# Differential attention: the weighted difference of the two softmaxes on GpSimd in two operations

## The chip, the cores and the metric

The kernel runs on one core of a Trainium2 chip. The metric is the time of one execution in microseconds (us) on the device. Three runs of the kernel before gave 3536.76, 3540.02 and 3542.56 us, the median is 3540.02.

The engines have short names in the rows: PE is TensorE (matmuls; PEld is its weight load), DVE is VectorE, ACT is ScalarE, POOL is GpSimd, SP starts most transfers.

## The reference

Two layers of a hybrid backbone run on 128 prompt tokens and 1024 latent tokens, all in float32. The second layer mixes a gated linear recurrence with differential attention: 4 heads, each with two sets of queries and keys of 64 columns, and values of 128 columns. Latent tokens see 128 context keys and their own 1024. What matters here:

```python
def diff_attention(q, keys, vals, lam):
    ...
    def block(qi):
        s = jnp.einsum('bhqpd,bhkpd->bhpqk', qi, keys).astype(F32) * scale
        p = jax.nn.softmax(s, axis=-1)
        w = p[:, :, 0] - lam * p[:, :, 1]
        return jnp.einsum('bhqk,bhkv->bhqv', w.astype(vals.dtype), vals)
...
    out_c = head_rms(o_c, p['diff_norm']) * (1.0 - lam_init)
```

lam is one number, worked out from the weights. Its value does not depend on the tokens.

## The kernel before

The layers run as stages, each on all 1152 tokens in nine tiles of 128. A scheduler writes the order of every engine's instructions from the program text, in which some parts are marked urgent. Each engine then works through its own order and waits for what the next instruction needs. An order is fixed: what stands behind a waiting instruction on its engine waits too.

The stage of the change is the attention of the latent tokens (`attention`, line 1303). It lasts from about 2310 to 2633 us and works on 32 blocks, numbered 1 to 32 here: eight blocks of 128 queries for each of four heads. One block goes like this.

- `scores` (L1328): for each of the two sets p, four matmuls into a PSUM tile s of 128x1024. There are two such tiles, so a set's scores can start when the exponential of the same set, one block earlier, has read its tile. The last 128 keys come from `tails` (L1313), for two blocks at once.
- `softmax` (L1199): VectorE takes the maximum of s (L1205) and joins that of the tail (L1207). ScalarE writes the exponentials into p, a tile of 128x1152, in two pieces, and adds each up on the way (L1214). The sums are joined and inverted (L1216, L1217). Neither set is divided by its sum yet. The tiles of the first set exist three times, those of the second twice.
- `weigh` (L1220): r2 becomes the factor for the second set, relative to the first (L1227). Then the combination: p1 = p2 * r2 + p1, on VectorE (L1228). The two softmaxes are urgent, these two lines are not.
- `values` (L1334), written in the program one block later: nine transposes of p1 (L1340) in three groups of three, each copied out of PSUM (ScalarE, VectorE, ScalarE), and nine matmuls with the values, each in two passes (L1344). `attn_tokens` scales the output by r1 (L1234).

After eight blocks (four at the end) the head's rows are normed and transposed back (`attn_out`, L1251), and written to DRAM or, for the last head, to x3.

Matmuls of the output projection are put between the blocks (`mix_group`, L205 to L207: three matmuls and one accumulation on VectorE, L1002, or a first copy on ScalarE). Their weights dl and half of their inputs mxl are made on GpSimd by a subtraction (L218). The weights of an adaLN projection are streamed meanwhile (`ada`, L384). When attention is done, the projection of the last head's rows runs (tile d), then the norm of nine token tiles and the last FFN.

The same `weigh` serves the prompt's 128 tokens (tag "p", tiles of 128x128).

Of the kernel before, what the change touches and what calls it, by code (L numbers as in the profile page):

```python
# [14 lines left out]
ALU = mybir.AluOpType  # L15
# [179 lines left out]
class Kern:  # L195
# [1024 lines left out]
    def weigh(self, pool, scores, r1, tag, bufs=2):  # L1220

        nc = self.nc
        r2 = pool.tile([P, 1], F32, tag="r2" + tag, name="r2")
        with self.urgent():
            p1, s1 = self.softmax(pool, scores(0), "p0", r1, bufs)
            p2, _ = self.softmax(pool, scores(1), "p1", r2)
        nc.vector.tensor_scalar(r2, r2, self.nlam, s1, ALU.mult, ALU.mult)  # L1227
        nc.vector.scalar_tensor_tensor(p1, p2, r2, p1, ALU.mult, ALU.add)  # L1228
        return p1

    def attn_tokens(self, ps, r1, ob, ss, junk):
# [394 lines left out]
```

## Time and profile before

| | |
|---|---|
| median of three runs | 3540.02 us |
| profiled execution | 3542.27 us |
| its span, first to last instruction | 3540.3 us |
| TensorE busy | 3333.9 us, 94% |
| VectorE busy | 1889.5 us, 53% |
| ScalarE busy | 1355.0 us, 38% |
| GpSimd busy | 880.6 us, 25% |
| mean granted clock of TensorE | 0.971 |

The shares are means over stages with different limits. A table of busy time by stretches tells what limits one of them; a list of waits tells which instruction ended an engine's idle time; the timeline gives the start and duration of single instructions. Durations of TensorE's matmuls overlap, so the distance from one start to the next is what they cost.

### The profile page before, as it was taken

To read this page: it belongs to the slowest core of one execution; us is meant where nothing else is said; L and a number is where in the kernel's file an instruction comes from. 1 tells how busy PE (TensorE), PEld (TensorE's weight loads), DVE (VectorE), ACT (ScalarE), POOL (GpSimd) and SP (SyncE) were. 2 spreads that over 40 slices of the span, in tenths; PEclk is the share of its full clock that TensorE was granted. 3 is DMA by queue.
4 is the path that set the end of the run, shared out by engine and by line. 5 is a ranking of instruction groups with operands and counts; after the bars stand their busy time and mean duration, and the time that the engine had idled before them with its cause. 6 is when DMAs were issued, how large, how long until landed. Compare 5 with 4: busy or idle time off the path is not lost.

```text
span 3540.3 us, 55870 instructions
## 1 busy us (share of the span) xinstructions
PE 3333.9 (94%) x23022; PEld 3022.1 (85%) x23022; DVE 1889.5 (53%) x3342; ACT 1355.0 (38%) x2414; POOL 880.6 (25%) x596
## 2 busy tenths in 40 slices
PE   5999999888699999999999999989988999999998
PEld 2999899756589999999988998957777999999997
DVE  5658997487662333433372246547777233343334
ACT  5334333453453222322254434446565322232223
POOL 2422320012242221322240003311125221232214
PEclk7999999999799999999999999989998999999999
DMA  6445334484231110111143324384123110111113
GB/s 216 140 138 153 115 108 142 174 295 157 71 96 39 46 37 30 54 42 42 31 148 115 122 82 133 104 285 114 51 83 108 48 36 25 54 48 47 37 30 137
DMA packets 272700, 348.08 MB, mean 98 GB/s; under 512 B 14354, under 2 KB 231597, under 8 KB 266302
## 3 DMA queue, kind: packets, MB, share of 16 engines
q1 hardware_dynamic: 269294, 334.82, 29.8%
q0 software_dynamic: 3152, 9.70, 0.9%
q8 instruction: 181, 2.97, 0.4%
q14 instruction: 73, 0.60, 0.1%
HBM read 266.58 MB, written 77.89 MB: 97 GB/s over the span
## 4 chain that ended last, share of the span: by engine, by line
PE 79%; DVE 8%; DMA 6%; ACT 3%; POOL 2%; issue 2%; SPq 0%; POOLq 0%; DVEq 0%; ACTq 0%
PE g L206 8%; PE g L207 8%; PE g L205 8%; PE a L205 7%; PE a L206 7%; PE a L207 7%; PE d L205 5%; PE d L206 5%; PE d L207 5%; DMA adaw<-in_ada_w 2%; PE b L1344 1%; DVE f L442 1%; PE s L1328 1%; PE w L205 1%; PE ad L384 1%
## 5 line engine op out<-in xcount | busy, mean ns | idle before, releaser
L206 PE MATMUL g<-hTl,whi 128*128 128x388 f32 (+2 forms) x1728 | 590.3, 342 | 2.3 <-POOL hTl L218 2.3
L205 PE MATMUL g<-hTh,whi 128*128 128x388 f32 (+2 forms) x1728 | 589.0, 341 | 2.3 <-ACT hTh L445 2.3
L207 PE MATMUL g<-hTh,wlo 128*128 128x388 f32 (+2 forms) x1728 | 588.1, 341 | 0.0
L206 PE MATMUL a<-hTl,whi 128*128 128x388 f32 (+2 forms) x1248 | 426.3, 342 | 3.4 <-POOL hTl L218 2.8
L205 PE MATMUL a<-hTh,whi 128*128 128x388 f32 (+2 forms) x1248 | 426.8, 342 | 0.9 <-ACT po L1430 0.5
L207 PE MATMUL a<-hTh,wlo 128*128 128x388 f32 (+2 forms) x1248 | 422.7, 341 | 0.0
L1002 DVE TENSOR_TENSOR acc<-d,acc 128x512 f32<-128x512 f32 x288 | 197.7, 688 | 330.7 <-PE d L207 329.2
L1104 POOL TENSOR_TENSOR ta<-ta,tg 128x386 f32<-128x386 f32 x132 | 135.6, 1027 | 922.4 <-ACT tg L1103 886.4
L205 PEld LDWEIGHTS g<-hTh,whi 128*128 128x128 f32 x1728 | 327.4, 189 | 6.7 <-ACT hTh L445 2.9
L206 PEld LDWEIGHTS g<-hTl,whi 128*128 128x128 f32 x1728 | 327.0, 189 | 6.7 <-POOL hTl L218 3.0
L207 PEld LDWEIGHTS g<-hTh,wlo 128*128 128x128 f32 x1728 | 326.9, 189 | 2.0
L205 PE MATMUL d<-dh,ah 128*128 128x512 f32 x792 | 312.6, 395 | 1.1 <-DVE acc L1002 1.1
L206 PE MATMUL d<-dl,ah 128*128 128x512 f32 x792 | 312.0, 394 | 0.0
L207 PE MATMUL d<-dh,al 128*128 128x512 f32 x792 | 311.9, 394 | 0.0
L476 ACT ACTIVATE tg<-g,cols,cols 128x386 f32<-128x386 f32 x132 | 88.8, 672 | 503.5 <-PE g L207 503.4
L218 POOL TENSOR_TENSOR wlo<-wraw,whi 128x1024 fp32r<-128x1024 f32 x90 | 218.3, 2426 | 160.6 <-ACT whi L211 159.7
L218 POOL TENSOR_TENSOR dl<-draw,dh 128x1024 fp32r<-128x1024 f32 x60 | 149.1, 2486 | 403.1 <-ACT dh L211 402.9
L206 PEld LDWEIGHTS a<-hTl,whi 128*128 128x128 f32 x1248 | 235.9, 189 | 11.3 <-POOL hTl L218 4.6
L205 PEld LDWEIGHTS a<-hTh,whi 128*128 128x128 f32 x1248 | 236.2, 189 | 9.7 <-issue 2.9
L477 DVE SCALAR_TENSOR_TENSOR tg<-g,cols,tg 128x386 f32<-128x386 f32 x132 | 81.8, 620 | 300.8 <-ACT tg L476 300.8
L207 PEld LDWEIGHTS a<-hTh,wlo 128*128 128x128 f32 x1248 | 235.8, 189 | 4.1 <-issue 1.6
L211 ACT ACTIVATE whi<-wraw 128x1024 fp32r<-128x1024 f32 x145 | 152.8, 1053 | 180.2 <-DMA wraw<-in_ffn_up 62.2
(429 smaller groups left out, 7050.3 us busy)
## 6 DMA issues: line engine op xcount, KB each, us to landing
adaw<-in_ada_w SPq DMA_DIRECT2D x48, 1024.0 KB
wraw<-in_ffn_up SPq DMA_DIRECT2D x88, 512.0 KB
draw<-in_ffn_down SPq DMA_DIRECT2D x44, 512.0 KB
wraw<-in_w_in_even SPq DMA_DIRECT2D x32, 512.0 KB
wraw<-in_w_in_odd SPq DMA_DIRECT2D x24, 512.0 KB
hgT<-po SPq DMA_DIRECT2D x16, 576.0 KB
ymid<-acc SPq DMA_DIRECT2D x18, 512.0 KB
y<-ymid SPq DMA_DIRECT2D x18, 512.0 KB
```

What stands on the lines that cost most here:

```text
L205: mm(out, lh, rh, start=start, stop=False)
L206: mm(out, lh, rl, start=False, stop=False)
L207: mm(out, ll, rh, start=False, stop=stop)
L211: eng.activation(out, in_, AF.Copy)
L218: eng.tensor_tensor(out, a, b, ALU.subtract)
L384: nc.tensor.matmul(ps[32 * n:32 * n + 32], self.csx[:, k, :], w[:, n, :], start=(k == 0), stop=(k == KD - 1))
L442: nc.vector.tensor_scalar(f[:, j], pt[:, 128 * j:128 * j + 128], mod[:, 1, g, k:k + 1], mod[:, 0, g, k:k + 1], ALU.mult, ALU.add)
L476: nc.scalar.activation(out, ps[:, 1:1 + n], AF.Identity, scale=w[1], bias=b)
L477: nc.vector.scalar_tensor_tensor(out, ps[:, 0:n], w[0], out, ALU.mult, ALU.add)
L1002: nc.vector.tensor_tensor(acc[:, i, s], ps, acc[:, i, s], ALU.add)
L1104: nc.gpsimd.tensor_tensor(ta, ta, tg, ALU.mult)
L1328: nc.tensor.matmul(s[:, k0:k0 + 512], q[:, p, 128 * t:128 * t + 128], kx[:, p, k0:k0 + 512], start=(x == 0), stop=(x == 1))
```

## The change

For the latent tokens (tag "s") the combination leaves VectorE. GpSimd multiplies the second set's exponentials by r2 in place, and then adds them to the first set's. The prompt's four combinations stay on VectorE.

```diff
         nc.vector.tensor_scalar(r2, r2, self.nlam, s1, ALU.mult, ALU.mult)
-        nc.vector.scalar_tensor_tensor(p1, p2, r2, p1, ALU.mult, ALU.add)
+        if tag == "s":
+            nc.gpsimd.tensor_scalar(p2, p2, r2, None, ALU.mult)
+            nc.gpsimd.tensor_tensor(p1, p1, p2, ALU.add)
+        else:
+            nc.vector.scalar_tensor_tensor(p1, p2, r2, p1, ALU.mult, ALU.add)
         return p1
```

Lines behind it move down by four: the transposes are L1344 in the kernel after, the value matmuls L1348, the scores L1332. The product is L1229, the sum L1230. The scheduler also writes a new order of the whole stage.

GpSimd before, from the end of the first adaLN piece to the end of attention; this is all that stands there. Numbers in names tell buffers apart.

```order
L218 TENSOR_TENSOR dl<-draw,dh 128x1024
L218 TENSOR_TENSOR mxl<-mxl,mxh 128x1152 x2
L218 TENSOR_TENSOR dl<-draw,dh 128x1024 x2
L218 TENSOR_TENSOR mxl<-mxl,mxh 128x1152
L218 TENSOR_TENSOR dl<-draw,dh 128x1024
L218 TENSOR_TENSOR mxl<-mxl,mxh 128x1152
L218 TENSOR_TENSOR dl<-draw,dh 128x1024
L218 TENSOR_TENSOR mxl<-mxl,mxh 128x1152
L218 TENSOR_TENSOR dl<-draw,dh 128x1024
```

GpSimd now, around blocks 16 and 17 (p_23452 is block 16's first set, p_23529 and p_23543 are block 17's two, p_23596 and p_23610 block 18's):

```order
L218 TENSOR_TENSOR dl<-draw,dh 128x1024
L1230 TENSOR_TENSOR p_23452<-p_23452,p_23466 128x1152
L218 TENSOR_TENSOR mxl<-mxl,mxh 128x1152
L218 TENSOR_TENSOR dl<-draw,dh 128x1024
L1229 TENSOR_SCALAR p_23543<-p_23543,r_23523 128x1152
L1229 TENSOR_SCALAR p_23610<-p_23610,r_23590 128x1152
L1230 TENSOR_TENSOR p_23529<-p_23529,p_23543 128x1152
L1230 TENSOR_TENSOR p_23596<-p_23596,p_23610 128x1152
```

Two products now stand ahead of block 17's sum, and three subtractions of the projection stand between block 16's product and block 17's. Further on, around block 28 (p_24325 and p_24339; block 29 is p_24400 and p_24414):

```order
L1229 TENSOR_SCALAR p_24264<-p_24264,r_24244 128x1152
L1230 TENSOR_TENSOR p_24250<-p_24250,p_24264 128x1152
L1229 TENSOR_SCALAR p_24339<-p_24339,r_24319 128x1152
L1229 TENSOR_SCALAR p_24414<-p_24414,r_24394 128x1152
L218 TENSOR_TENSOR mxl<-mxl,mxh 128x1152
L1230 TENSOR_TENSOR p_24325<-p_24325,p_24339 128x1152
L1230 TENSOR_TENSOR p_24400<-p_24400,p_24414 128x1152
L1229 TENSOR_SCALAR p_24481<-p_24481,r_24461 128x1152
```

Two products and a subtraction stand between block 27's sum and block 28's.

TensorE now, ahead of block 17's transposes (p_23529); the scores are the first set's of block 20:

```order
L1317 MATMUL b<-kh,q 128x128
L1317 MATMUL b<-kl,q 128x128
L1332 MATMUL s<-kh,q 128x512
L1332 MATMUL s<-kl,q 128x512
L1332 MATMUL s<-kh,q 128x512
L1332 MATMUL s<-kl,q 128x512
L1344 MATMUL b<-ident,p_23529 128x128 x6
L1332 MATMUL s<-kh,q 128x512
L1332 MATMUL s<-kl,q 128x512
```

The transposes stand right behind that set of scores. Block 28's follow the first set of block 31 with three more matmuls between:

```order
L1332 MATMUL s<-kh,q 128x512
L1332 MATMUL s<-kl,q 128x512
L1332 MATMUL s<-kh,q 128x512
L1332 MATMUL s<-kl,q 128x512
L207 MATMUL w<-dh,mxl 128x512
L205 MATMUL w<-dh,mxh 128x512
L206 MATMUL w<-dl,mxh 128x512
L207 MATMUL w<-dh,mxl 128x512
L1344 MATMUL b<-ident,p_24325 128x128 x6
```

The end of attention, TensorE before, from the last block's transposes (p_24580) to the transposes of the output:

```order
L1340 MATMUL b<-ident,p_24580 128x128 x6
L205 MATMUL w<-dh,mxh 128x512
L206 MATMUL w<-dl,mxh 128x512
L207 MATMUL w<-dh,mxl 128x512
L1344 MATMUL b<-v,w 128x128 x9
L205 MATMUL w<-dh,mxh 128x512
L206 MATMUL w<-dl,mxh 128x512
L207 MATMUL w<-dh,mxl 128x512
L205 MATMUL w<-dh,mxh 128x512
L206 MATMUL w<-dl,mxh 128x512
L207 MATMUL w<-dh,mxl 128x512
L1251 MATMUL b<-ident,ob 128x128 x4
```

The same place now, from the last block's third group of transposes (p_24611):

```order
L1344 MATMUL b<-ident,p_24611 128x128 x3
L1348 MATMUL b<-v,w 128x128 x6
L205 MATMUL w<-dh,mxh 128x512
L206 MATMUL w<-dl,mxh 128x512
L207 MATMUL w<-dh,mxl 128x512
L1348 MATMUL b<-v,w 128x128 x3
L205 MATMUL w<-dh,mxh 128x512
L206 MATMUL w<-dl,mxh 128x512
L207 MATMUL w<-dh,mxl 128x512
L1255 MATMUL b<-ident,ob 128x128 x4
```

The groups w are the output projection. Ahead of the last block's transposes there are now nine such matmuls behind block 31's, where there were three. Behind them there were 30, the last ones between those of d; now there are six.

## Rows read from the trace of the kernel before

**Rows 1.** Busy time by stretches (us from the span's start)

```profile
core 0: us, PE busy (x) PEld busy (x) DVE busy (x) ACT busy (x) POOL busy (x), PEclk, DMA share, GB/s
2340.00:2620.00 280.00, 258.75 (x1585) 211.70 (x1583) 211.44 (x431) 167.57 (x413) 28.27 (x15) 0.98 0.35 103
2640.00:2680.00 40.00, 24.77 (x89) 16.45 (x87) 39.08 (x79) 32.17 (x62) 27.08 (x12) 0.72 0.57 197
```

**Rows 2.** Groups of instructions, 2310 to 2640 us: busy us, mean ns | idle before

```profile
L1205 DVE TENSOR_REDUCE smx<-s 128x1 f32<-128x1024 f32 x64 | 77.5, 1218 | 15.1 <-PE s L1328 14.8
...
L1214 ACT ACTIVATE p<-s,smx 128x1024 f32<-128x1024 f32 x64 | 70.4, 1099 | 0.0
...
L1228 DVE SCALAR_TENSOR_TENSOR p<-p,r,p 128x1152 f32<-128x1152 f32 x32 | 49.8, 1557 | 0.5
...
L1214 ACT ACTIVATE p<-xt,smx 128x128 f32<-128x128 f32 x64 | 25.4, 397 | 29.0 <-DVE smx L1207 28.7 <-DVE ssm L1216 0.2
...
L1214 ACT ACTIVATION_READ_ACCUMULATOR p<-s,smx 128x1 f32 x64 | 12.4, 193 | 0.0
```

**Rows 3.** Waits, 2320 to 2625 us: total us, times, longest

```profile
ACT p L1214 <- DVE smx L1207: 28.7, 17, 3.7
...
PE b L1340 <- ACT w L211: 5.3, 7, 1.9
...
PE b L1340 <- DVE ob L1234: 3.6, 2, 3.1
...
PE b L1344 <- ACT w L211: 2.3, 4, 0.6
...
PE b L1344 <- DVE w L215: 1.5, 4, 0.7
...
PE w L205 <- DVE acc L1002: 0.7, 2, 0.4
```

**Rows 4.** GpSimd's groups, whole span, shapes apart: busy us, mean ns | idle before

```profile
L213 POOL TENSOR_SCALAR qs<-qx 128x256 fp32r<-128x256 f32 x34 | 31.6, 930 | 10.0 <-DMA qx<-in_cache_diff_k 7.2
L1185 POOL TENSOR_TENSOR qx<-qx,qr 128x256 f32<-128x256 f32 x32 | 27.8, 870 | 365.0 <-PE a L206 240.0 <-DVE qr L1183 107.7 <-PE p L1292 9.7
L218 POOL TENSOR_TENSOR mxl<-mxl,mxh 128x1152 fp32r<-128x1152 f32 x10 | 27.4, 2752 | 48.9 <-ACT mxh L211 44.4 <-DMA mxl<-mixT 4.4
...
L389 POOL MEMSET adag<- 128x512 f32 x6 | 3.2, 540 | 60.5 <-DVE adab L400 60.5
```

**Rows 5.** Timeline, a subtraction beside a combination: start us, us

```profile
2525.73 2.64 POOL L218 TENSOR_TENSOR mxl<-mxl,mxh 128x1152 fp32r<-128x1152 f32 x1 [18.37 <-ACT mxh L211]
...
2526.80 2.80 DVE L1228 SCALAR_TENSOR_TENSOR p<-p,r,p 128x1152 f32<-128x1152 f32 x1
```

**Rows 6.** Timeline, combinations and first transposes of blocks 5, 29, 32

```profile
2363.44 1.42 DVE L1228 SCALAR_TENSOR_TENSOR p<-p,r,p 128x1152 f32<-128x1152 f32 x1
...
2388.06 0.87 PE L1340 MATMUL b<-ident,p 128*128 128x128 f32 x6
...
2601.43 2.37 DVE L1228 SCALAR_TENSOR_TENSOR p<-p,r,p 128x1152 f32<-128x1152 f32 x1
...
2604.34 0.38 PE L1340 MATMUL b<-ident,p 128*128 128x128 f32 x2
...
2622.26 1.41 DVE L1228 SCALAR_TENSOR_TENSOR p<-p,r,p 128x1152 f32<-128x1152 f32 x1
...
2624.48 0.49 PE L1340 MATMUL b<-ident,p 128*128 128x128 f32 x3
```

**Rows 7.** Timeline, two of TensorE's last scores

```profile
2614.33 0.40 PE L1328 MATMUL s<-kh,q 128*128 128x512 f32 x1
2614.57 0.40 PE L1328 MATMUL s<-kl,q 128*128 128x512 f32 x1
```

**Rows 8.** VectorE's accumulations, 2620 to 2700 us; a load on the chain

```profile
L1002 DVE TENSOR_TENSOR acc<-w,acc 128x512 f32<-128x512 f32 x14 | 9.6, 685 | 4.6 <-PE w L207 4.6
...
2634.32 6.84 DMA y<-ybuf
```

## The prediction

> **What bounds the kernel now.** I read the busy table by stretches first. From 2340 to 2620 us, where most of the attention blocks run, TensorE is busy 258.75 of 280 us (92%) and VectorE 211.44 (76%); GpSimd is at 28.27, nearly free [rows 1]. So this stretch is bound by TensorE, and all that anything there can give back is the 21 us in which TensorE is idle. From 2640 to 2680 it is the other way: VectorE 39.08 of 40 us, TensorE 24.77 [rows 1]. Each of the 32 blocks (128 queries of one head) costs VectorE two maxima of 1218 ns and the combination of 1557 ns, 49.8 us in all for the 32 combinations; none of the reasons for which TensorE waited names the combination [rows 2, 3]. TensorE's listed waits from 2320 to 2625 us go to ScalarE's evictions and exponentials, to DMA, and for 3.6 + 1.5 + 0.7 = 5.8 us to VectorE (the scaled output, the copy of transposed weights, the accumulation) [rows 3].
>
> Why the combination isn't waited for: the order of the program puts the transposes of a block well behind it. Block 5's combination ends at 2363.44 + 1.42 = 2364.86, its first transpose starts at 2388.06, 23.2 us later. That is the largest of 32 gaps, the smallest is 0.54 us in block 29 (2601.43 + 2.37 to 2604.34) [rows 6]. Taken so from the timeline for every block, seven gaps are under 3.7 us: blocks 1 (1.54), 21 (1.44), 27 (2.64), 28 (2.56), 29 (0.54), 31 (1.47) and 32 (0.81); 25 are longer.
>
> **The change, part by part.**
> *VectorE loses 32 combinations*, 49.8 us of 211, so it falls from 76% to some 58% of the stretch. One of them ran 2.80 us beside a subtraction on GpSimd [rows 5], where an undisturbed one takes 1.42 [rows 6]; all 32 together are 49.8 - 32 x 1.41 = 4.7 us above that. What remains on VectorE there reads PSUM or one operand of size, so I expect the collisions to go with it. The relief shows only where TensorE waited for VectorE: between 0 and 5.8 us, and some more where ScalarE's exponentials had waited for the maximum. I take -4 us.
>
> *GpSimd gets a product and a sum per block.* The sum has a row of its own size: 128x1152, 2752 ns mean, 2.64 us alone [rows 4, 5]. The product with a column as factor has none. Its nearest rows: a TENSOR_SCALAR of 256 columns, 930 ns mean; a MEMSET of 512 columns, 540 ns [rows 4]. At the memset's rate 1152 columns cost 1.2 us; with 930 ns scaled by 1152/256 they cost 4.2 us. The row of 256 is as slow as the sum of 256 columns (870 ns), so I take about the sum's price, 2.5 us, and keep 1.2 and 4.2 for the range. The pair is then 5.1 us (3.8 to 6.8) in place of 1.41, that is 3.7 us more between a block's softmax and its transposes. In throughput that fits: 32 x 5.1 = 163 us beside 28 us of other work, in 300 us. At 4.2 us it would be 32 x 6.8 = 218 us, and still fit.
> The Trainium skill (GPSIMD Engine Reference, Engine selection) says that GpSimd runs a one-input operation at roughly line rate, and only two-input ones at half of VectorE's speed. An estimate by it and the clock of 1.2 GHz in that page is 1152 / 1.2 = 0.96 us for the product; the waits priced at +8 below would then be near +3, and the sum -4. The row of 256 columns in 930 ns does not look like it, though it writes runs of 64 and may be slow for that.
>
> *What the order does with it.* The program's order is made anew, and it moves most transposes back. Where the gap was long, 3.7 us more is hidden behind the matmuls of other blocks and of the output projection. Three places are left, read from the order of GpSimd and TensorE in front of this text. (1) Before block 17's sum stand the products of blocks 17 and 18, so its transposes wait for block 18's softmax and then for a product and a sum: 5.1 us. TensorE's order keeps them behind the first scores of block 20, which wait for an exponential that comes one exponential after block 18's last one. That is 1.10 + 0.40 us for the two pieces of an exponential and 2 x 0.19 for reading their sums [rows 2] and about 4 x 0.24 = 0.95 us of scores [rows 7], 2.8 us together. Short by 2.3 us. (2) Before block 28's sum stand the products of 28 and 29 and a subtraction of 1152 columns: 2.5 + 2.64 + 2.64 = 7.8 us from block 29's softmax, against the same 2.8: short by 5.0 us. (3) Block 32: its combination starts at 2622.26 and its transposes at 2624.48 [rows 6], 2.2 us; the pair needs 5.1, so it is 2.9 short, and six more projection matmuls stand ahead, 6 x 0.24 = 1.4 us. Short by 1.5. Sum 8.8; some of it will stand where TensorE had other waits before, so I take +8 us. Bounds: 0 if the product is at 1.2 us and all is covered. At the other end, with the order of before, the seven short gaps lack 2.2 + 2.3 + 1.1 + 1.1 + 3.2 + 2.2 + 2.9 = 15 us.
>
> *The end of the stage.* Before, 30 matmuls of the projection (pieces w) follow block 32's transposes, in ten groups of three, each with an accumulation on VectorE; now six do. So eight accumulations of 685 ns, which follow each other in about 0.6 us, leave the stretch in which VectorE is the bound [rows 1, 8]: -4.8 us at most. They are paid ahead, with 24 x 0.24 = 5.8 us of TensorE's time, part of which fills the waits of (3). The load that starts when attention ends (6.84 us, on the chain [rows 8]) still has 54 matmuls over it. I take -3 us, with bounds -4.8 and +3.
>
> *The rest.* GpSimd also makes the low halves of the projection's operands, and these now queue behind products that wait for a softmax. Before, it stood idle for 18.37 us ahead of one of them [rows 5]; I price that inside +8. SP issues the same DMAs in almost the same order, and outside this stage the order is the same but for small swaps up to the first convolutions of the last FFN.
>
> **Sum.** -4 + 8 - 3 = +1 us on the profiled execution, 3542.3 to 3543.3 us. That execution lies 2.25 us above the median of 3540.02, so the forecast is 3541 us, no change to be seen: a measurement here tells about 0.2% (7 us) from none.
>
> **The rivals.** *Relief wins (faster):* VectorE at 58% answers sooner everywhere. The 5.8 us go whole, and half of TensorE's two largest waits on ScalarE too (5.3 + 2.3 = 7.6 us), since ScalarE itself had waited 28.7 us for the maximum [rows 3]; the new waits are covered but for 1 us, and the tail gives 3. -5.8 - 3.8 + 1 - 3 = -12 us, 3528 us. For it: the combination stands in front of evictions in VectorE's queue. Against it: TensorE is 92% busy, and most of its waits are on ScalarE's own queue, where nothing gets lighter.
> *The pair is late (slower):* GpSimd's product and sum end after TensorE's order wants the transposes, at the start of head 3 and in the last six blocks above all. Those stalls add 15 us by the gaps above, with little relief in exchange: 3555 us. It decides from a product above about 3 us: with 4.2 us the three places lack 2 x 1.7 us more at the first two and 1.7 at the third, and blocks 18 to 20 and 26 to 31, with gaps of 0.5 to 9 us in the old order, join. For it: sums that stand behind the next block's product. Against it: the order leaves more matmuls ahead of most transposes than before.
> *It is hidden whole:* the order covers everything and VectorE's relief meets no wait. 3540 us, within the forecast's range.
>
> **Chances and range.** Forecast with the hidden case 50% (its own range 3534 to 3548 us); slower rival 28%; faster rival 20%; something not thought of 2%. The range reaches most of the way into both rivals: 3529 to 3559 us. Faster by over 0.2%: 0.20; within: 0.49; slower: 0.31, the last with 3% from the forecast's own upper edge.
>
> **What would show it.** In the profile after: VectorE's busy time some 50 us lower, GpSimd's some 160 us higher; the product's duration, 2.5 us or not; a wait of TensorE's transposes for GpSimd's sum that wasn't there, of 2 us at block 17 and 5 us at block 28, and little in the other blocks; TensorE's waits on VectorE halved; VectorE's crowded stretch after attention 3 us shorter. I am wrong if the product lies far from 2.5 us, if the transposes wait for GpSimd in many blocks (slower), or if TensorE's idle time in the stage falls by more than 8 us (faster).

## The result and the profile after

The changed kernel takes 3594.13 us (3590.83 to 3599.83, 4 runs) against 3538.39 us for the kernel before (4 runs): 1.0159 times as long, 95% interval 1.0143 to 1.0175. It is 56 us slower, where no change was forecast, and outside the range.

Where the time is, is seen first on the page's lines of busy time. Before, and after:

```profile
PE 3333.9 (94%) x23022; PEld 3022.1 (85%) x23022; DVE 1889.5 (53%) x3342; ACT 1355.0 (38%) x2414; POOL 880.6 (25%) x596
```

```profile
PE 3347.6 (93%) x23022; PEld 3032.3 (84%) x23022; DVE 1889.4 (53%) x3310; ACT 1356.7 (38%) x2414; POOL 1065.7 (30%) x660
```

The spans are 3540.3 and 3588.8 us. TensorE runs the same 23022 instructions; it is idle 241.2 us instead of 206.4 (+34.8), and the same instructions take 13.7 us longer: together the 48.5 us between the two spans. (The medians lie 56 us apart: the profiled execution of before is slower than its median, that of after faster.) VectorE has 32 instructions fewer, the combinations of [rows 2], and is busy just as long. That line contradicts the forecast, which had its busy time 50 us lower.

The stretches of [rows 1], after:

```profile
core 0: us, PE busy (x) PEld busy (x) DVE busy (x) ACT busy (x) POOL busy (x), PEclk, DMA share, GB/s
2340.00:2620.00 280.00, 236.98 (x1384) 193.62 (x1377) 180.36 (x339) 144.17 (x352) 169.37 (x65) 0.93 0.32 93
2640.00:2680.00 40.00, 33.16 (x200) 26.43 (x198) 24.41 (x52) 18.01 (x43) 17.90 (x7) 0.98 0.08 27
```

In the first stretch TensorE is idle 43 us instead of 21, at a granted clock of 0.93 instead of 0.98. From 2640 to 2680 us attention is still running.

Groups of instructions of the stage after, 2310 to 2690 us (busy us, mean ns | idle before), to be laid beside [rows 2 and 4]:

```profile
L1229 POOL TENSOR_SCALAR p<-p,r 128x1152 f32<-128x1152 f32 x32 | 102.5, 3204 | 114.1 <-DVE r L1227 70.4 <-ACT p L1214 22.0 <-PE w L207 11.7
L1230 POOL TENSOR_TENSOR p<-p,p 128x1152 f32<-128x1152 f32 x32 | 85.4, 2675 | 1.4
L1205 DVE TENSOR_REDUCE smx<-s 128x1 f32<-128x1024 f32 x64 | 77.6, 1216 | 15.4 <-PE s L1332 15.3
...
L1216 DVE TENSOR_TENSOR ssm<-ssm 128x1 f32<-128x1 f32 x64 | 49.7, 777 | 40.0 <-ACT p L1214 39.5
...
L1245 DVE TENSOR_TENSOR ob<-ob,o8r 128x1024 f32<-128x1024 f32 x3 | 7.3, 2444 | 0.1
```

And one line of before, 2310 to 2640 us:

```profile
L1216 DVE TENSOR_TENSOR ssm<-ssm 128x1 f32<-128x1 f32 x64 | 12.0, 187 | 27.0 <-ACT p L1214 26.7
```

The product takes 3.20 us (forecast 2.5), the sum 2.68 (2.64). The maxima, which read PSUM (where the matmuls write), are untouched. The line to stop at is L1216. It is the smallest work on VectorE, one number per partition: a softmax's row sum comes in two halves, and L1216 adds them. Its 64 instructions went from 12.0 to 49.7 us, so they took back 37.7 of the 49.8 us that the combinations had left. Much of the rest is in other operations with two tensors in SBUF, where the kernel keeps its tiles: the scaling of a finished head's rows (L1245), three instructions, takes 7.3 us instead of 3.7. The timeline of the joins shows why (start us, us):

```profile
2509.31 2.37 POOL L218 TENSOR_TENSOR dl<-draw,dh 128x1024 fp32r<-128x1024 f32 x1
...
2509.82 1.86 DVE L1216 TENSOR_TENSOR ssm<-ssm 128x1 f32<-128x1 f32 x1 [3.56 <-ACT p L1214]
...
2511.64 3.22 POOL L1229 TENSOR_SCALAR p<-p,r 128x1152 f32<-128x1152 f32 x1
...
2511.80 2.83 DVE L1216 TENSOR_TENSOR ssm<-ssm 128x1 f32<-128x1 f32 x1
```

Both joins end with GpSimd's running instruction (2511.68 against 2511.68, 2514.63 against 2514.86). So do all 28 joins of this trace that last over 0.4 us: the 20 beside a sum or a subtraction to 0.03 us of an end, the 8 beside a product 0.22 us ahead of it. The median join takes 160 ns, the longest 2830.

How a held join reaches TensorE shows at 2560 us:

```profile
2551.31 2.51 DVE L1216 TENSOR_TENSOR ssm<-ssm 128x1 f32<-128x1 f32 x1
...
2553.93 2.46 DVE L1216 TENSOR_TENSOR ssm<-ssm 128x1 f32<-128x1 f32 x1
...
2560.27 0.80 PE L205 MATMUL w<-dh,mxh 128*128 128x512 f32 x1 [5.68 <-DVE acc L1002]
```

Two joins keep VectorE for 5 us, the maxima and the accumulation behind them come later, and TensorE waits 5.68 us for the accumulation. With short joins in the same order (e1 below) that wait is 2.55 us.

TensorE's waits after, 2310 to 2680 us (total, times, longest), beside [rows 3]:

```profile
PE s L1332 <- ACT p L1214: 17.2, 8, 6.9
PE w L205 <- DVE acc L1002: 11.4, 8, 5.7
...
PE w L207 <- POOL mxl L218: 2.0, 2, 1.8
PE b L1344 <- POOL p L1230: 2.0, 1, 2.0
```

The wait that the forecast priced, transposes for GpSimd's sum, is there once, 2.0 us. The large ones have other names: scores that wait for exponentials (2.1 us before), and the projection waiting for its accumulation on VectorE.

The two longest, 6.0 and 6.9 us, stand where a head ends. First the end of the first head before, on TensorE: own-key scores, then what runs until the next scores.

```profile
2422.85 0.27 PE L1313 MATMUL b<-kl,q 128*128 128x128 f32 x1
2422.96 0.44 PE L205 MATMUL w<-dh,mxh 128*128 128x512 f32 x1
2423.86 0.88 PE L1340 MATMUL b<-ident,p 128*128 128x128 f32 x6 [0.46 <-DVE ob L1234]
...
2427.42 2.28 PE L1344 MATMUL b<-v,w 128*128 128x128 f32 x18 [0.58 <-ACT w L211]
...
2431.03 0.39 PE L207 MATMUL w<-dh,mxl 128*128 128x512 f32 x1
2431.26 0.40 PE L1328 MATMUL s<-kh,q 128*128 128x512 f32 x1
```

The same place after:

```profile
2429.12 0.28 PE L1317 MATMUL b<-kl,q 128*128 128x128 f32 x1
...
2429.98 0.39 PE L207 MATMUL w<-dh,mxl 128*128 128x512 f32 x1
2436.34 0.80 PE L1332 MATMUL s<-kh,q 128*128 128x512 f32 x1 [5.98 <-ACT p L1214]
2436.94 0.63 PE L1332 MATMUL s<-kl,q 128*128 128x512 f32 x1
```

ScalarE there, before and then after:

```profile
2424.26 1.28 ACT L262 ACT_TABLE_LOAD   x1
...
2429.07 1.09 ACT L1214 ACTIVATE p<-s,smx 128x1024 f32<-128x1024 f32 x1
```

```profile
2429.40 1.28 ACT L262 ACT_TABLE_LOAD   x1
2430.69 0.30 ACT L262 ACTIVATE o8sd<-ss,eps 128x8 f32<-128x8 f32 x1
2430.90 0.58 ACT L211 ACTIVATE xt<-b 128x512 f32<-128x512 f32 x1
2433.41 1.28 ACT L1214 ACT_TABLE_LOAD   x1 [1.93 <-DVE smx L1207]
...
2435.11 1.09 ACT L1214 ACTIVATE p<-s,smx 128x1024 f32<-128x1024 f32 x1
```

The scores need a PSUM tile that an exponential must free, and the exponential stands behind the norm of the finished head, with a table load (1.28 us, where ScalarE goes from the exponential to the square root and back) on each side of it. From the first load to that exponential it is 5.7 us, 1.9 of them a wait for VectorE's maximum. Before, it was hardly shorter, 4.8 us, but TensorE had 12 transposes, 18 value products and 9 projection matmuls over it. After, four projection matmuls are left: the new order had moved the transposes and value products behind these scores, out of the pair's way. The two score matmuls shown behind the gap take 0.80 and 0.63 us; the one shown of before takes 0.40. The stretch behind the gap, after, shows the clock:

```profile
2436.00:2440.00 4.00, 3.65 (x9) 2.89 (x10) 2.42 (x6) 1.77 (x6) 0.00 (x0) 0.50 0.00 0
```

The granted clock is 0.50, that is 1.2 GHz of 2.4, behind 6 us in which TensorE did nothing; from 2420 to 2430 us it was 0.83, from 2440 on 0.99. So this gap is paid a second time in slower matmuls.

### The profile page after: what moved, and what is told of

The parts are those of the page before. It is cut to its first block, busy times and chain, and to the rows that moved or that the text cites. A ratio compares the mean times of both kernels' runs of the same rounds, so it can differ in the third digit from the quotient of the medians.

```text
span 3588.8 us, 56035 instructions
## 1 busy us (share of the span) xinstructions
PE 3347.6 (93%) x23022; PEld 3032.3 (84%) x23022; DVE 1889.4 (53%) x3310; ACT 1356.7 (38%) x2414; POOL 1065.7 (30%) x660
## 4 chain that ended last, share of the span: by engine, by line
PE 77%; DVE 9%; DMA 6%; ACT 3%; issue 2%; POOL 2%; SPq 0%; POOLq 0%; ACTq 0%; DVEq 0%
PE g L206 8%; PE g L207 8%; PE g L205 8%; PE a L205 7%; PE a L207 7%; PE a L206 7%; PE d L205 5%; PE d L206 5%; PE d L207 5%; DMA adaw<-in_ada_w 2%; DVE f L442 1%; PE b L1348 1%; PE w L205 1%; PE s L1332 1%; DVE acc L1002 1%
```

## The experiments

Each time is a median, given with the difference from the kernel before as measured beside it (3535.5 to 3537.3 us), the ratio and its 95% interval.

**The joins with one operand.** The add of two columns becomes a sum over a row of two; nothing else moves. Once in the changed kernel (e1), once in the kernel before (e2).

```diff
-            nc.vector.tensor_tensor(sm[:, 0:1], sm[:, 0:1], sm[:, 1:2], ALU.add)
+            nc.vector.tensor_reduce(sm[:, 2:3], sm[:, 0:2], AX.X, ALU.add)
```

> Changed kernel, the join of a set's two sums (one element per partition, two operands in SBUF) written as a reduction of two neighbouring columns (one operand). The order of all engines stays the same. Theory A (VectorE's two-operand joins wait until GpSimd's running instruction ends, 37 us more in the 64 joins, and the stage pays for it): the joins fall from 777 ns to about 160 ns mean, the kernel to 3545 us, +-10. Rival B (the pair is late for the transposes, and the new order is worse): joins may get shorter, but the kernel stays above 3580 us.

> Kernel before with the same reduction in place of the two-operand join, order all but unchanged. A and B: 3538 us +-5, since few joins met a GpSimd instruction there (187 ns mean).

e1: 3579.76 us, +43.8 (ratio 1.0124, 1.0110 to 1.0138). e2: 3537.34, +1.4 (1.0002, 0.9993 to 1.0011). In e1 the joins are short:

```profile
L1216 DVE TENSOR_REDUCE ssm<-ssm 128x1 f32<-128x2 f32 x64 | 9.7, 151 | 46.4 <-ACT p L1214 45.9
```

The mechanism holds, its size does not: the joins are worth 12 to 14 us here, and 44 us are left. Theory A as the whole cause falls; the time lies on rival B's bound of 3580. Only the joins are freed here: the three scalings of a head's rows still take 6.7 us.

**GpSimd's work added, VectorE's kept (e3).** The combination stays on VectorE, and GpSimd does the same two operations on the used-up second set; nobody reads the result.

```diff
         nc.vector.scalar_tensor_tensor(p1, p2, r2, p1, ALU.mult, ALU.add)
+        if tag == "s":
+            nc.gpsimd.tensor_scalar(p2, p2, r2, None, ALU.mult)
+            nc.gpsimd.tensor_tensor(p2, p2, p2, ALU.add)
         return p1
```

> Kernel before with its combination on VectorE, and then the same two GpSimd operations of 128x1152 per block on the used-up second set, whose result nobody reads; only the next exponential into that tile waits for them. A: slower by 25 to 50 us, joins and combinations lengthened by GpSimd's instructions. B: within 8 us of before, since no transposes wait for GpSimd.

3559.6 us, +23.7 (1.0067, 1.0053 to 1.0081), joins 747 ns. A GpSimd that TensorE doesn't wait for costs 24 us, just under A's 25 to 50 and far above B's 8, but in an order of its own: this run can't tell joins from order.

**No combination at all (e6).** For the latent tokens p1 is returned as it is; the second set is left out of the result.

```diff
         if tag == "s":
-            nc.gpsimd.tensor_scalar(p2, p2, r2, None, ALU.mult)
-            nc.gpsimd.tensor_tensor(p1, p1, p2, ALU.add)
+            pass
```

> No combination on any engine for the latent tokens: the second set's exponentials are computed and left out of the result. It shows the most that taking it from VectorE can be worth. A and B: 3520 to 3538 us; A further: the joins at about 190 ns mean.

3537.04 us, +1.1 (1.0005, 0.9994 to 1.0015). VectorE is busy 45 us less (1844.3 us), and nothing is won. But this run too has an order of its own, so alone it is no bound; h2 below, with VectorE as free and the order of before, gains nothing either.

**Order and place, apart.** A table of numbers fixes the issue order of every engine, with the combination itself free to be placed by the scheduler; the constraint sets order alone and waits for nothing.

```diff
-        Kern(tc, aps, outs).run()
+        k = Kern(tc, aps, outs)
+        k.pair = set()
+        k.run()
+        force(tc, k.pair, ORDER)
```

f1 is the kernel before in the order of the changed one; f2 is e1 in the order of before; f3 is the changed kernel itself in the order of before.

> The combination stays on VectorE in one operation as before, and every other instruction of every engine is issued in the order of the changed kernel. What e1 left of the loss, 43.8 us, has two candidates. Theory C (the order is not to blame; the later end of the combination on GpSimd is): the time is that of before, 3536 us, within 6. Rival D (the other order of TensorE, ScalarE and VectorE costs by itself, with fast combinations too): 3565 to 3582 us, and TensorE waits on p of ScalarE and acc of VectorE at the same places as in the changed kernel. Between 3545 and 3562 both hold a share.

> The two operations on GpSimd with the one-operand joins of e1, and every other instruction of every engine in the order of before. Theory C: the lateness stays, 3570 to 3585 us. Rival D: without the other order only the late pair is left, which my prediction priced at 8 us (15 with a product of 3.2 us): 3540 to 3555 us. Joins about 150 ns in both.

> The changed kernel itself, two-operand joins and all, in the order of before. It gives the price of the joins a second time: Theory A (a join on VectorE with two operands lasts until the running instruction of GpSimd ends) has the joins at 600 to 800 ns mean and this run 8 to 20 us above f2. Rival: the 14 us of e1 were an effect of that order alone, and this run lies within 4 us of f2.

| over before, us | order of before | order of the changed kernel |
|---|---|---|
| combination on VectorE | 0 | f1: +57.8 (1.0165, 1.0149 to 1.0180) |
| pair on GpSimd, one-operand joins | f2: +29.5 (1.0082, 1.0067 to 1.0097) | e1: +43.8 |
| pair on GpSimd, two-operand joins | f3: +38.4 (1.0112, 1.0097 to 1.0127) | changed kernel: +56 |

Neither theory was right alone. The new order with the combination on VectorE costs as much as the whole change, more than D's 3565 to 3582; and the pair in the old order costs 29.5 us, between the two forecasts. The effects don't add. The new order suits the pair better than the combination on VectorE (by 14 us), but it is the worse one for both: the pair too is 14 us better off in the order of before, and the changed kernel 18. The joins cost 8.9 us in the old order and about 12 in the new (their mean in f3 is 693 ns).

One thing f1 does not separate: its combinations stand where the scheduler put them in an order made without them, 14 of 32 right ahead of a maximum (11 before). So 57.8 us is the price of the order with the combination in it. The order with no combination at all was not run.

The traces agree on the stage itself, from its first score to the last transposes of its output: 313.9 us before, 367.1 changed, 367.5 in f1, 355.4 in e1, 346.9 in f2, 352.0 in f3. What stands ahead of the stage varies by up to 9 us between executions in the same order (first score at 2319.4 us before, 2310.4 in f2).

TensorE's waits in f1 (2310 to 2690 us), then in f2 (2300 to 2680):

```profile
PE s L1330 <- ACT p L1214: 22.5, 11, 6.4
PE w L205 <- DVE acc L1002: 7.8, 6, 2.4
```

```profile
PE b L1346 <- POOL p L1231: 30.5, 9, 6.7
```

f1 shows the waits of the changed kernel, without the pair on GpSimd. f2 shows the wait that I had forecast for the changed kernel, at nine places, 30.5 us in all, about the size of the loss. The longest is that of block 1, whose sum stands behind block 2's product:

```profile
2327.38 3.20 POOL L1230 TENSOR_SCALAR p<-p,r 128x1152 f32<-128x1152 f32 x1 [11.73 <-ACT p L1214]
2330.96 3.20 POOL L1230 TENSOR_SCALAR p<-p,r 128x1152 f32<-128x1152 f32 x1 [0.38 <-DVE r L1228]
2334.13 2.61 POOL L1231 TENSOR_TENSOR p<-p,p 128x1152 f32<-128x1152 f32 x1
```

**The two operations in halves (f4)**, in the order of the changed kernel.

```diff
-            nc.gpsimd.tensor_scalar(p2, p2, r2, None, ALU.mult)
-            nc.gpsimd.tensor_tensor(p1, p1, p2, ALU.add)
+            for x in (slice(0, 576), slice(576, 1152)):
+                nc.gpsimd.tensor_scalar(p2[:, x], p2[:, x], r2, None, ALU.mult)
+                nc.gpsimd.tensor_tensor(p1[:, x], p1[:, x], p2[:, x], ALU.add)
```

> The changed kernel in its own order, each of the two GpSimd operations cut into two of 576 columns. Theory A: a join waits for the end of one instruction, so the longest joins beside these operations fall from 2.8 us to about 1.6, the mean from 777 ns to 400 to 550, and the time falls by 3 to 10 us from that of the changed kernel, 3594 to 3584 to 3591, less what two more starts of an instruction per pair add. Rival E (the join waits while GpSimd has work of this kind queued, however it is cut): the longest joins stay at 2.8 us or grow, and the mean stays at 700 ns or more.

3583.64 us, +47.3 (1.0139, 1.0118 to 1.0159): 8 to 10 us below the changed kernel, though the intervals overlap.

```profile
L1216 DVE TENSOR_TENSOR ssm<-ssm 128x1 f32<-128x1 f32 x64 | 29.8, 466 | 42.4 <-ACT p L1214 42.1
```

The mean falls from 777 to 466 ns, and the longest join beside the halves is 1.42 us; the two longest of all, 2.56 and 2.38, lie beside subtractions that were not cut. A join waits for one instruction, as theory A has it.

**The order's second part alone (k2).** f1 with the order of before up to the own-key scores of blocks 21 and 22.

```diff
-        force(tc, k.pair, ORDER)
+        force(tc, k.pair, ORDER_BEFORE_THEN_AFTER)
```

> The combination on VectorE in one operation; up to the own-key scores of blocks 21 and 22 every engine in the order of before, from there in the order of the changed kernel. In f1, with the changed order throughout, the copy of those own-key scores came 26.1 us later than before (2557.60 against 2531.53 us), about half of its loss of 58 us. Rival D1 (the changed order loses wherever it stands, at each head end and wherever TensorE's queue has no work ahead): 3560 to 3572 us. Rival D2 (the second part only pays for work that the first part had or had not done): within 10 us of before, 3536 to 3546.

3568.17 us, +30.8 (1.0093, 1.0078 to 1.0108): D1. The second part alone costs about half of f1's loss; the first alone was not run. The two longest waits of scores for exponentials, 3.3 and 3.1 us, stand in the second part:

```profile
PE s L1330 <- ACT p L1214: 9.2, 7, 3.3
```

**Product and sum kept together (h1)**, f2 with GpSimd's queue changed so that no other operation stands between a product and its sum.

```diff
 L1230 TENSOR_SCALAR p_22424<-p_22424,r_22404 128x1152
-L1230 TENSOR_SCALAR p_22461<-p_22461,r_22441 128x1152
 L1231 TENSOR_TENSOR p_22410<-p_22410,p_22424 128x1152
+L1230 TENSOR_SCALAR p_22461<-p_22461,r_22441 128x1152
 L1231 TENSOR_TENSOR p_22447<-p_22447,p_22461 128x1152
```

> f2 (pair on GpSimd, one-operand joins, order of before) with each sum moved right behind its own product in GpSimd's queue, so that no product of another block and no subtraction stands between. Theory F (TensorE waits for the sums because they stand behind other GpSimd work): in f2's nine waits of 30.5 us, 3.5 at block 1, 4.9 at 2509 us, 1.0 at 2538 and about 3.2 at 2615 are time behind other work, 12 us together: 3550 to 3558 us. Rival G (the pair's own 5.9 us are too long wherever they stand): 3561 to 3570 us.

3564.43 us, +27.1 (1.0078, 1.0061 to 1.0094). TensorE's waits, 2300 to 2680 us:

```profile
PE b L1346 <- POOL p L1231: 17.1, 8, 3.6
PE w L206 <- POOL dl L218: 5.4, 1, 5.4
PE w L207 <- POOL mxl L218: 5.2, 2, 3.4
```

The transposes' wait falls by 13.4 us, near the 12 that theory F had worked out. Of these, 4.2 come back as waits for the projection's low halves, which now stand behind the sums (3.1 and 3.3 us in f2). The time is that of G, only 2.4 us under f2. The stage itself is 6.5 us shorter in the traces (340.4 against 346.9 us), about half of what the wait lost; medians that vary by several us don't settle how much of it reaches the time. Most of f2's loss stays with each sum right behind its product, as G has it.

**The product alone (h2)**, f2 without the sum; the first set is left out of the result.

```diff
-            nc.gpsimd.tensor_scalar(p2, p2, r2, None, ALU.mult)
-            nc.gpsimd.tensor_tensor(p1, p1, p2, ALU.add)
+            nc.gpsimd.tensor_scalar(p1, p2, r2, None, ALU.mult)
```

> f2 without the sum: GpSimd writes the scaled second set alone, and the first set is left out of the result; order of before, one-operand joins. GpSimd's part is 3.2 us in place of 5.9. Theory C (what f2 loses, 29.5 us, is the lateness of the weights): of its nine waits (6.7, 6.0, 4.9, 3.6, 2.2, 2.2, 2.1, 1.9, 1.0) each loses 2.65 us or more, which leaves under 9 us, less what the queue gives: 3537 to 3546 us. Rival H (a busy GpSimd slows others whatever waits for it): half the loss or more stays, 3550 us or above.

3539.01 us, +1.7 (1.0005, 0.9995 to 1.0014); TensorE waits for it 2.6 us in all, three times. The stage takes 313.6 us, as before (313.9). In the old order 3.2 us on GpSimd per block are free and 5.9 cost 29.5 us. What f2 loses is lateness; rival H falls, though the pair's work on GpSimd is also nearly halved here. And VectorE without the combination (1843.6 us busy), in the order of before and with one-operand joins, wins nothing.

**Forms on VectorE beside GpSimd (m1).**

```diff
+            for i in range(6):
+                nc.gpsimd.tensor_scalar(z, x, m, None, ALU.mult)
+            for i in range(12):
+                nc.vector.tensor_copy(o[:, 0:512], a[:, 0:512])
```

> Nothing of the reference is computed. Twelve instructions of one form on VectorE: alone, beside six products on GpSimd (TENSOR_SCALAR 128x1152 by a column), beside six sums (TENSOR_TENSOR 128x1152). Nine forms: add of two columns, sum of two neighbouring columns, column times column, copy of 512, scaled 128 from PSUM, maximum over 1024 of PSUM, PSUM + SBUF of 512, SBUF + SBUF of 512, and the combination of 1152. Theory A (an operation of VectorE with two tensors in SBUF waits until GpSimd's running instruction ends): the add of two columns, SBUF + SBUF and the combination take 2 to 3.5 us each beside either, the other six the same as alone within 10%. Rival I (the wait hangs on an operation being tiny, or on its kind of result): the sum of two columns or column times column are slowed too, or the large SBUF + SBUF is slowed in proportion only.

Beside the products (busy us, mean ns):

```profile
L118 DVE SCALAR_TENSOR_TENSOR o<-a,b 128x1152 f32<-128x1152 f32 x12 | 32.5, 2712 | 0.4
...
L115 DVE TENSOR_TENSOR o<-a,b 128x512 f32<-128x512 f32 x12 | 24.2, 2015 | 0.4
L103 DVE COPY o<-a 128x512 f32<-128x512 f32 x12 | 22.4, 1865 | 0.4
...
L112 DVE TENSOR_TENSOR o<-pt,b 128x512 f32<-128x512 f32 x12 | 8.3, 690 | 0.4
...
L94 DVE TENSOR_TENSOR o<-a,b 128x1 f32<-128x1 f32 x12 | 3.7, 377 | 0.0
...
L97 DVE TENSOR_REDUCE o<-a 128x1 f32<-128x2 f32 x12 | 0.8, 147 | 0.0
```

Alone these take 1419, 692, 427, 691, 156 and 153 ns. Two tensors in SBUF are slowed; a tensor in PSUM, a sum over neighbouring columns, a column times a column (217 alone, 204 beside) and the maximum are not. Of the twelve adds of two columns one waits beside the products, 2.86 us, and three beside the sums, up to 2.59: once one is through, the next follow. That is fewer than theory A had. Against theory A stands the copy of 512 columns: one operand, and 427 ns become 1865 (1570 beside the sums). "Two tensors" is too narrow a rule.

The Trainium skill (SBUF — State Buffer, section "SBUF: two separate sides") states that a VectorE operation with two SBUF inputs, or in a faster two-port mode, and a GpSimd operation take the same pair of ports, for a whole instruction each. By that rule the joins and the copy wait and the PSUM forms don't: the traces agree, 2.83 us for a single add included.

**The head's end without table loads (n1, n2).** The norm's square root becomes a copy, in the changed order (n1) and in that of before (n2).

```diff
-        nc.scalar.activation(sd, ssq, AF.Sqrt, scale=1.0 / n, bias=self.eps[0:ssq.shape[0]])
+        nc.scalar.activation(sd, ssq, AF.Copy, scale=1.0 / n)
```

> f1 (combination on VectorE, everything issued in the order of the changed kernel) with the square root in the norm at the end of a head replaced by a copy, so that ScalarE loads no other table there: six loads of 1.28 us fewer; the norm's values are then not the reference's. In f1 TensorE stands idle 6.1, 6.4 and 3.3 us at the three head ends, in front of scores that wait for exponentials behind these loads. Theory D3 (the order took away the transposes and value products that covered this chain, so it lies open): f1's 3594 us fall by 5 to 9 us more than n2 falls against before. Rival D4 (what the order costs lies elsewhere, and another wait ends there at once): n1 within 3 us of f1 less what n2 gains.

> The same replacement in the order of before, the control. Theory D3: there the chain lies beside transposes, value products and projection matmuls, so the six loads are worth 0 to 3 us: 3533 to 3537 us. Rival D4: 4 us or more, as in n1.

n1: 3580.22 us, +44.7 (1.0127, 1.0113 to 1.0141), so 13.1 below f1. n2: 3529.98, -5.5 (0.9979, 0.9970 to 0.9988). By the medians the loads cost 7.6 us more in the changed order, within D3's 5 to 9; by the length of the stage it is 4.1 (367.5 to 359.4 against 313.9 to 309.9). With intervals of some 5 us either way that is not settled, and the control gained what D4 had for it, not D3's 0 to 3 us. And of the three long waits only the first becomes shorter (6.07 to 3.76 us; 6.42 to 5.95, 3.31 to 3.29): at the second, VectorE's maxima and combination hold the exponentials in place of the loads. Most of the gain is in TensorE's busy time, 3352.3 us in f1 and 3341.5 in n1, at a mean granted clock of 0.966 and 0.970. The loads are a part of what lies open at the heads' ends, not the bulk of what the order costs.

## Why the prediction was wrong

- *What bounds the stage*: right. TensorE bounds it, and the combination was not waited for. e6 (+1.1) and, in the order of before, h2 (+1.7) put VectorE's relief at about 0; I had -4, with 0 as a bound. "Relief wins" falls.
- *"What remains on VectorE there reads PSUM or one operand of size, so I expect the collisions to go with it"*: failed. I had put these collisions at nothing. What remained were adds of one element from two places in SBUF, and larger two-operand work such as the head's scaling. I looked at size, and even an add of one element per partition was held: the joins gained 37.7 us of busy time, and cost 8.9 us in the old order and about 12 in the new. My own [rows 5], a combination held for a GpSimd operation's length, showed the price of one collision; 64 GpSimd operations more should have been set against every two-operand instruction left.
- *The product at 2.5 us*: 3.20, within its bounds; the pair is 5.9 us, not 5.1. The Trainium skill's "roughly line-rate" (GPSIMD Engine Reference, Engine selection), 0.96 us by my estimate, does not hold for this form: it is slower than the sum.
- *"What the order does with it", +8*: this is the step that failed by most. With the joins out of the way (e1) pair and order together still cost 43.8 us. The waits that I counted at blocks 17, 28 and 32 are not there; the only one is 2.0 us, at block 27; the new order did cover the pair. I counted only what that cover gives and put what it takes at nothing: the transposes and value products that it moved back had filled TensorE's time, at the heads' ends most visibly (6.1, 6.4 and 3.3 us of idle time in f1). f1 prices the new order at 57.8 us with the combination on VectorE; against f3, the changed kernel in the old order, the new order costs 18 us. Those three gaps are a part of it; how the rest comes about stays open.
- *My bound for the order of before, 15 us*: f2 measured 29.5. The seven short gaps of [rows 6] were taken with each pair alone; behind other GpSimd work there are nine, and up to 6.7 us. "The pair is late" named the right sign and, in f2, the right mechanism; in the changed kernel it is not what costs. I had it decide from a product above about 3 us: at 3.20 us it does in the old order (+29.5) and does not in the new (2.0 us of wait).
- *The end of the stage, -3*: gone the other way. From the last combination to the end it was 3540.3 - 2623.67 = 916.6 us [rows 6]; now the last sum starts at 2666.6 and takes some 2.6, which leaves 919.6.
- *"The rest"*: held. TensorE waits 2.0 us for the projection's low halves, no more than before (2.5 us, 1.8 and 0.7).

Still open: which part of the new order costs how much, and what it costs with no combination in it. Neither the order of TensorE alone nor that of another engine alone was run. Of f1's loss, 32 us are idle time of TensorE (238.7 against 206.4), 18 us are its instructions taking longer; 20 us of the idle time are scores that wait for exponentials (22.5 against 2.1).

## What to carry over

Where a scheduler writes the order, a change of engine is two changes; hold the order fixed and price each alone, and read what moved back as work that something else was covered by. Here the old order forced on the changed kernel (f3) would have saved 18 of the 56 us. Before putting work on an idle GpSimd, list VectorE's instructions with two operands in SBUF, the one-element ones too: each may be held for as long as a GpSimd instruction lasts. And remove the operation altogether first, in the same order: e6 and h2 show that there was nothing to win.

## What was not expected of the hardware

An add of one element per partition lasted 2.83 us beside a GpSimd product of 3.22, and 151 ns as a sum over two neighbouring columns. GpSimd's product by a column (3.20 us for 1152) is slower than its sum of two tensors (2.68). A copy of 512 columns within SBUF is held like an operation with two operands: 427 ns alone, 1865 beside the products.
